# Input projection of a hybrid decoder layer: outputs with tokens on partitions, half of the contraction by Strassen's block scheme

## The chip, the cores and the metric

The kernel runs on one core of a Trainium2 chip. The metric is the device time of one execution in microseconds (us). Before the change the median of three runs is 696.79 us (696.76 to 697.26).

A core has five engines that work beside each other and meet at semaphores: TensorE (PE, matmuls; its weight loads are listed as PEld), VectorE (DVE), ScalarE (ACT), GpSimd (POOL) and SyncE (SP, which issues most transfers here). Matmul results go to PSUM, which has eight banks of 128 partitions x 512 fp32 words.

## The reference

One decoder layer on 256 tokens of width 2048, in fp32. The input projection is by far the largest product: 2048 x 11264 weights.

```python
h = rms_norm(x, norm_g)                                    # x: 256 x 2048
proj = h @ w_in                                            # 2048 x 11264
q, k, v, z_a, u_b, v_b, z_b, g_a, g_b = jnp.split(proj, cuts, axis=-1)   # seven of 1024, two of 2048
q, k = rms_norm(q, q_norm_g), rms_norm(k, k_norm_g)        # per head of 128, 8 heads
att = moba_attention(q, k, v)                              # 256 tokens: one block, causal softmax
y_a = (att * silu(z_a)) @ w_proj_a                         # 1024 x 2048
sgu = spatial_gating(gelu(u_b), gelu(v_b), ...)            # u * (W_s norm(v) + b), chunks of 128
y_b = (sgu * silu(z_b)) @ w_proj_b                         # 1024 x 2048
merged = sigmoid(g_a) * y_a + sigmoid(g_b) * y_b
return x + merged @ w_out                                  # 2048 x 2048
```

## The kernel before

**The weight stream.** All weights are laid out on the host as one stream of 120 granules of 128 x 2048 words (1 MB), in the order in which they are used (`schedule`). Granule i is loaded into a raw buffer by SP's queue (`load`, L96) three granules ahead, and split two granules ahead (`split`): ACT casts it to fp32r, the high half (wh, L120), and DVE subtracts the high half from the raw word, the low half (wl, L121), in two pieces of 1024 words. Every product of fp32 precision is then three fp32r products: low x high, high x high and high x low.

**Two kinds of granules.** For vb, v, q, k and out a *natural* granule holds 4 k tiles x 512 columns. The halves of x (or of the merged rows) are the stationary operand, the weights are moving, and the output has tokens on partitions (`mm_nat`, L233): 24 matmuls of 512 columns per granule, into two banks, one for each half of the tokens. For ub, zb, za, ga, gb and the two projections a *transposed* granule holds 16 k tiles x 128 columns. The weights are stationary, and x's two halves, side by side, are moving (`mm_tr`): one matmul of 512 columns with wh (L241) and one of 256 with wl (L243) for each k tile. The output then has columns on partitions, and ACT and DVE add its two parts (`tr_sum`, L248 and L250).

**x and its norm.** The layer's norm is not applied to x itself. x arrives transposed (`load_x`, L134), is multiplied by its gain and split into halves (`split_x`, L164 and L165). The rms of each token (rstd; R as a row) is applied after the product: as ACT's scale for natural outputs, by DVE (L372) for transposed ones.

**Order.** The stream runs vb, ub, v, q, k, zb, za, then 16 rounds of one tile of ga, one of gb and one of the projections, then out in four chunks of 512 columns. Work beside the stream (squares, transposes of q and k, scores, softmax, attention, spatial mixing) is hung on granule numbers with `at`. The framework turns this into one queue for each engine. It orders the instructions by priority and readiness, so an engine's order can differ from the text; each engine then executes its queue in order. Only the first splits are ordered by hand (`manual_schedule`).

**Buffers.** Three raw buffers, five half granules of wh and of wl; 14 general buffers of 2048 words; four banks of PSUM for accumulators and four for the rest.

Of the kernel before, what the change touches and what calls it, by code (L numbers as in the profile page):

```python
# [24 lines left out]
H = 8  # L25
# [3 lines left out]
WORDS = 2048  # L29
# [4 lines left out]
COLS = {"q": 0, "k": 1024, "v": 2048, "za": 3072, "ub": 4096, "vb": 5120, "zb": 6144,  # L34
        "ga": 7168, "gb": 9216}


def schedule():
    s = []

    def nat(name, c):
        s.extend(("nat", name, c, q) for q in range(4))

    def tr(name, j):
        s.append(("tr", name, j, 0))

    for c in range(2):
        nat("vb", c)
    for j in range(8):
        tr("ub", j)  # L50
    for name in ("v", "q", "k"):
        for c in range(2):
            nat(name, c)
    for name in ("zb", "za"):
        for j in range(8):
            tr(name, j)
    for j in range(16):
        tr("ga", j)
        tr("gb", j)
        s.append(("proj", "proj", j, 0))  # L60
    for c in range(4):
        nat("out", c)
    return s
# [3 lines left out]
def hybrid_layer_kernel(  # L67
# [6 lines left out]
    bs: bass.AP,  # L74
# [7 lines left out]
    big = ctx.enter_context(tc.tile_pool(name="big", bufs=14))  # L82
    wpool = ctx.enter_context(tc.tile_pool(name="wpool", bufs=3))
    work = ctx.enter_context(tc.tile_pool(name="work", bufs=2))
    small = ctx.enter_context(tc.tile_pool(name="small", bufs=4))
    ps_acc = ctx.enter_context(tc.tile_pool(name="ps_acc", bufs=4, space=bass.MemoryType.PSUM))
    ps_sd = ctx.enter_context(tc.tile_pool(name="ps_sd", bufs=4, space=bass.MemoryType.PSUM))
# [5 lines left out]
    raw, wh, wl = {}, {}, {}  # L93
# [3 lines left out]

    def load(i, pieces=1):
        if i >= NG:
            return  # L100
        raw[i] = wpool.tile([P, WORDS], F32, tag="raw", name=f"raw{i}")
        n = WORDS // pieces
        for a in range(pieces):
            load_piece(i, a * n, (a + 1) * n)

    HW = WORDS // 2

    def split(i, pieces=1, hs=range(2), js=None):
        if i >= NG:
            return  # L110
        n = HW // pieces
        for h in hs:
            if (i, h) not in wh:
                wh[i, h] = wpool.tile([P, HW], F32R, tag="wh", bufs=5, name=f"wh{i}_{h}")
                wl[i, h] = wpool.tile([P, HW], F32R, tag="wl", bufs=5, name=f"wl{i}_{h}")
            a, b = wh[i, h], wl[i, h]
            for j in js or range(pieces):
                sl = slice(j * n, (j + 1) * n)
                r = raw[i][:, h * HW + j * n:h * HW + (j + 1) * n]
                nc.scalar.copy(a[:, sl], r)  # L120
                nc.vector.tensor_tensor(b[:, sl], r, a[:, sl].bitcast(F32), op=ALU.subtract)  # L121

# [8 lines left out]
    xs = []

    def load_x(k0, k1):
        nc.sync.dma_start(xt[k0 // 8][:, k0 % 8:(k1 - 1) % 8 + 1, :],  # L134
                          xT[:, NV + k0 * S:NV + k1 * S].rearrange("p (k t) -> p k t", t=S))

    raw[0] = wpool.tile([P, WORDS], F32, tag="raw", name="raw0")
    nc.sync.dma_start(xv[:, 0:NV + S], xT[:, 0:NV + S])
    load_piece(0, 0, 512)
    nc.sync.dma_start(xv[:, NV + S:], xT[:, NV + S:NV + 2 * S])  # L140
# [8 lines left out]
    for i in range(4):  # L149
        xs.append(slot(F32R, f"xs{i}").rearrange("p (k c) -> p k c", c=512))  # L150

    warm = const.tile([P, 512], BF16, name="warm")
    nc.vector.memset(warm, 0.0)
    ps_w = ps_sd.tile([P, 512], F32, tag="sd", name="ps_w")
# [3 lines left out]
    def split_x(i, kks=range(4)):  # L158
        for kk in kks:
            k = 4 * i + kk  # L160
            src = x_k(k)
            g = vec[:, k:k + 1]
            hi = xs[i][:, kk, 0:S]
            nc.scalar.activation(hi, src, AF.Copy, scale=g)  # L164
            nc.vector.scalar_tensor_tensor(xs[i][:, kk, S:], src, g, hi.bitcast(F32),  # L165
                                           op0=ALU.mult, op1=ALU.subtract)
# [3 lines left out]
    ones = const.tile([P, 1], F32, name="ones")  # L170
    nc.gpsimd.memset(ones, 1.0)
    mhalf = const.tile([P, 8], F32, name="mhalf")
    nc.gpsimd.memset(mhalf, -0.5)
    tri_f = work.tile([P, 4, P], F32, tag="t2k", bufs=6, name="tri_f")
# [5 lines left out]
    wb = slot(F32, "wb").rearrange("p (a h t) -> p a h t", a=2, t=P)  # L180
    ws, bsb = wb[:, 0], wb[:, 1]

    def load_mix():
        nc.sync.dma_start(ws, wsT)
        nc.gpsimd.affine_select(out=ws, in_=ws, pattern=[[0, H], [1, P]], base=0,
                                channel_multiplier=-1, compare_op=ALU.is_ge, fill=0.0)
        nc.sync.dma_start(bsb, bass.AP(tensor=bs.tensor, offset=bs.offset,
                                       ap=[[0, P], [P, H], [1, P]]))
# [3 lines left out]
    sq = [slot(F32, f"sq{i}").rearrange("p (k t) -> p k t", t=S) for i in range(2)]  # L192
    ssum = work.tile([P, 2, S], F32, tag="t2k", bufs=6, name="ssum")

    def squares(i):
        if i == 0:
            nc.scalar.activation(sq[0][:, 0:2, :], xv[:, NV:].rearrange("p (k t) -> p k t", t=S), AF.Square)
            nc.scalar.activation(sq[0][:, 2:, :], xt[0][:, 2:, :], AF.Square)
        else:
            nc.scalar.activation(sq[i], xt[i], AF.Square)  # L200
        nc.vector.reduce_sum(ssum[:, i, :], sq[i].rearrange("p k t -> p t k"), axis=AX.X)
# [21 lines left out]
    def mm_nat(acc, lhs, i, q, by_row=False):  # L223
# [3 lines left out]
        for kk, m in order:  # L227
            k = 4 * q + kk
# [314 lines left out]
```

## Time and profile before

| | us |
|---|---|
| median of three runs | 696.79 |
| lowest and highest run | 696.76, 697.26 |
| span of the profiled execution | 695.3 |
| the profiled execution's own time | not listed apart from its span |
| PE busy in the span | 689.0 |
| DVE busy | 443.9 |
| ACT busy | 352.2 |
| mean transfer rate | 192 GB/s |

The span runs from the first to the last instruction of one execution; what lies around it is not in the profile. Busy times of the engines overlap, so they don't add up to the span. Matmuls are pipelined and their ends are modelled: a group's mean duration is longer than the distance from one matmul to the next, and this distance is the price in a full stream. The chain that ended last is followed back from the last instruction, at each step to what released it.

### The profile page before, as it was taken

Reading aid. Unit: us, or ns where it says so; the run is one execution under the profiler, and the core shown is the slowest. Engines: PE = TensorE matmul, PEld = TensorE weight load, DVE = VectorE, ACT = ScalarE, POOL = GpSimd, SP = SyncE. Lnnn points to the kernel's source line nnn. Section 1 sums busy time; section 2 is a strip of 40 time slices with the busy share of each in tenths; the row PEclk is TensorE's granted clock in tenths of the full one; section 3 lists DMA queues with packets and bytes.
Section 4 is the critical chain, followed back from the end, with each engine's and each line's share of the span. In section 5 each row is a group of like instructions: output and inputs, shape, how many; then the busy total and the mean of one; then the engine's idle time right before and its main releaser. Section 6 shows DMA issues by size and latency. Waiting matters only on the chain.

```text
span 695.3 us, 9323 instructions
## 1 busy us (share of the span) xinstructions
PE 689.0 (99%) x3638; PEld 591.6 (85%) x3638; DVE 443.9 (64%) x604; ACT 352.2 (51%) x522; POOL 22.6 (3%) x26
## 2 busy tenths in 40 slices
PE   8999999999999999999999999999999999999997
PEld 5888888888888889888888888888888888888886
DVE  5988555546566685866666666666666666654551
ACT  6854443344444496855644554455445445534330
POOL 1022000000111100000000000000000000000000
PEclk9999999999999999999999999999999999999999
DMA  8766554554555545445555555555545555557730
GB/s 309 296 249 235 182 187 176 182 186 181 196 184 189 182 154 209 156 153 199 194 182 181 186 186 201 195 201 184 182 182 187 194 199 200 190 181 247 251 138 30
DMA packets 21788, 133.77 MB, mean 192 GB/s; under 512 B 2417, under 2 KB 2929, under 8 KB 7025
## 3 DMA queue, kind: packets, MB, share of 16 engines
q1 hardware_dynamic: 20592, 131.09, 52.2%
q10 hardware_dynamic: 1152, 2.10, 1.0%
q8 instruction: 28, 0.46, 0.3%
q14 instruction: 16, 0.12, 0.0%
HBM read 131.08 MB, written 2.10 MB: 192 GB/s over the span
## 4 chain that ended last, share of the span: by engine, by line
PE 99%; DMA 1%; ACT 0%; DVE 0%; SPq 0%; DVEq 0%; issue 0%
PE acc_out L233 13%; PE acc_gb L241 8%; PE acc_ga L241 8%; PE acc_vb L233 7%; PE acc_v L233 6%; PE acc_q L233 6%; PE acc_k L233 6%; PE acc_ga L243 4%; PE acc_gb L243 4%; PE acc_ub L241 4%; PE acc_zb L241 4%; PE acc_za L241 4%; PE acc_pb L241 4%; PE acc_pa L241 4%; PE acc_pa L243 2%; PE acc_pb L243 2%
## 5 line engine op out<-in xcount | busy, mean ns | idle before, releaser
L121 DVE TENSOR_TENSOR wl<-raw,wh 128x1024 fp32r<-128x1024 f32 (+1 forms) x250 | 294.4, 1182 | 203.4 <-ACT wh L120 200.4
L120 ACT CAST wh<-raw 128x1024 fp32r<-128x1024 f32 (+1 forms) x250 | 253.2, 1018 | 302.1 <-PE acc_ga L241 44.5
L241 PE MATMUL acc_ga<-xs,wh 128*128 128x512 f32 x256 | 89.5, 391 | 0.0
L241 PE MATMUL acc_gb<-xs,wh 128*128 128x512 f32 x256 | 89.5, 391 | 0.0
L233 PE MATMUL acc_out<-wh,mT 128*128 128x512 f32 x256 | 78.8, 390 | 0.0
L243 PE MATMUL acc_gb<-xs,wl 128*128 128x256 f32 x256 | 71.8, 281 | 0.0
L243 PE MATMUL acc_ga<-xs,wl 128*128 128x256 f32 x256 | 71.8, 281 | 0.0
L241 PEld LDWEIGHTS acc_gb<-xs,wh 128*128 128x128 f32 x256 | 47.9, 187 | 10.4
L241 PEld LDWEIGHTS acc_ga<-xs,wh 128*128 128x128 f32 x256 | 47.9, 187 | 10.4
L233 PEld LDWEIGHTS acc_out<-wh,mT 128*128 128x128 f32 x256 | 48.0, 188 | 9.9
L233 PE MATMUL acc_out<-wl,mT 128*128 128x512 f32 x128 | 49.9, 390 | 0.0
L243 PEld LDWEIGHTS acc_gb<-xs,wl 128*128 128x128 f32 x256 | 48.5, 190 | 0.0
L243 PEld LDWEIGHTS acc_ga<-xs,wl 128*128 128x128 f32 x256 | 48.5, 190 | 0.0
L241 PE MATMUL acc_zb<-xs,wh 128*128 128x512 f32 x128 | 45.5, 399 | 0.0
L241 PE MATMUL acc_ub<-xs,wh 128*128 128x512 f32 x128 | 45.3, 399 | 0.0
L241 PE MATMUL acc_pb<-zbT,wh 128*128 128x512 f32 x128 | 45.1, 391 | 0.0
L241 PE MATMUL acc_pa<-zaT,wh 128*128 128x512 f32 x128 | 45.1, 391 | 0.0
L241 PE MATMUL acc_za<-xs,wh 128*128 128x512 f32 x128 | 44.6, 393 | 0.0
L233 PE MATMUL acc_vb<-wh,xs 128*128 128x512 f32 x128 | 41.2, 404 | 1.3 <-ACT wh L120 1.3
L233 PE MATMUL acc_v<-wh,xs 128*128 128x512 f32 x128 | 39.9, 393 | 0.0
L233 PE MATMUL acc_k<-wh,xs 128*128 128x512 f32 x128 | 39.6, 391 | 0.0
L233 PE MATMUL acc_q<-wh,xs 128*128 128x512 f32 x128 | 39.5, 390 | 0.0
(142 smaller groups left out, 1056.1 us busy)
## 6 DMA issues: line engine op xcount, KB each, us to landing
raw<-in_w SPq DMA_DIRECT2D x115, 1024.0 KB, 4.8
raw<-in_w SPq DMA_DIRECT2D x9, 512.0 KB, 7.9
xres<-in_x ACTq DMA_DIRECT2D x8, 256.0 KB, 7.1
out<-o SPq DMA_DIRECT2D x7, 256.0 KB, 6.5
xt<-in_xT SPq DMA_DIRECT2D x3, 512.0 KB, 8.2
raw<-in_w SPq DMA_DIRECT2D x2, 256.0 KB, 4.6
wb<-in_wsT SPq DMA_DIRECT2D x1, 512.0 KB, 5.7
wb<-in_bs SPq DMA_DIRECT2D x1, 512.0 KB, 7.5
```

Of the source, the lines that this page charges most:

```text
L120: nc.scalar.copy(a[:, sl], r)
L121: nc.vector.tensor_tensor(b[:, sl], r, a[:, sl].bitcast(F32), op=ALU.subtract)
L233: nc.tensor.matmul(acc[m], a, b[i, h][:, o:o + 512], start=(k == 0 and n == 0), stop=(k == KT - 1 and n == 2))
L241: nc.tensor.matmul(acc, wh[i, h][:, o:o + P], r, start=(kk == 0), stop=False, skip_group_check=True)
L243: nc.tensor.matmul(acc[:, 0:S], wl[i, h][:, o:o + P], r[:, 0:S], start=False, stop=(kk == nk - 1), skip_group_check=True)
```

## The change

The input projection is rebuilt. All outputs of it, and those of the projections, now have tokens on partitions.

- **Quads.** A quad is 1024 output columns: q, k, v, za, vb, ub, zb, and four quads of g, each with 512 columns of ga and 512 of gb. It has eight granules; granule kp holds k tiles kp and kp + 8 for two column blocks of 512, as blocks 12, 11, 22, 21 (first digit the half of k, second the column block). With two halves of the tokens there are four accumulators, one bank each. A *direct* granule does all eight block products (`direct`). In all quads but q, granules kp 0 to 3 are done by `seven`: seven block products, with four sums of weight blocks (t, built on DVE in `split`) and four forms of x blocks (`forms`). Four of the seven go to banks E and are combined by `early`, three go on in the accumulators L; `final` adds both. Quads take their granules in the order 4, 5, 0, 1, 6, 2, 3, 7. E and L change places from quad to quad.
- **Split.** A Strassen granule takes three additions on DVE (1024, 512 and 512 words), then casts and subtractions of 1536 and of 2048 words. Others take one cast and one subtraction of 2048.
- **Norm.** q is computed on x times its gain and scaled afterwards. In the meantime x is normalised, and all other quads use normalised x. For the statistics x is loaded a second time with tokens on partitions; ACT squares it.
- **Order.** q, k, v, za, vb, ub, zb, then four rounds of a g quad and four granules of the projections (512 columns), then out.
- **Work beside it.** Norms of heads use ACT's accumulators (`sums`). The softmax's denominator is applied with the gate, after attention. The gated results (`turn_z`) and the merged rows (`turn_m`) are transposed on PE.

```diff
+SK = (0, 1, 2, 3)
+MIXED = (4, 5, 0, 1, 6, 2, 3, 7)
+    quad("q", 0, PLAIN)
+    for name in ("k", "v", "za", "vb", "ub", "zb"):
+        quad(name, 0, MIXED)
     for c in range(4):
-        nat("out", c)
+        quad("g", c, MIXED)
+        s.extend(("proj", "proj", c, q, q) for q in range(4))
+    for c in range(4):
+        s.extend(("out", "out", c, q, q) for q in range(4))
...
+        t = wpool.tile([P, WORDS], F32, tag="raw", bufs=4, name=f"t{i}")
+        two = t[:, 0:2 * B].rearrange("p (a n) -> p a n", a=2)
+        nc.vector.tensor_tensor(two, r[:, B:3 * B].rearrange("p (a n) -> p a n", a=2),
+                                r[:, None, 0:B].to_broadcast([P, 2, B]), op=ALU.add)
+        nc.vector.tensor_tensor(t[:, 2 * B:3 * B], t[:, 0:B], r[:, 2 * B:3 * B], op=ALU.add)
+        nc.vector.tensor_tensor(t[:, 3 * B:], t[:, 2 * B:3 * B], r[:, 3 * B:], op=ALU.add)
+        wh[i] = wpool.tile([P, 3 * B], F32R, tag="whp", bufs=2, name=f"whp{i}")
+        wl[i] = wpool.tile([P, 3 * B], F32R, tag="wlp", bufs=2, name=f"wlp{i}")
+        halve(wh[i], wl[i], r[:, B:])
+        th[i] = wpool.tile([P, WORDS], F32R, tag="wh", bufs=3, name=f"th{i}")
+        tl[i] = wpool.tile([P, WORDS], F32R, tag="wl", bufs=3, name=f"tl{i}")
+        halve(th[i], tl[i], t)
...
+    xn = [slot(F32, f"xnat{m}") for m in range(2)]
+    for m in range(2):
+        nc.sync.dma_start(xn[m], x[m * P:(m + 1) * P, :])
...
+    def normalise(i):
+        src = xt[i]
+        nc.vector.tensor_tensor(src, src, R[:, None, :].to_broadcast([P, 8, S]), op=ALU.mult)
...
+        nc.vector.tensor_tensor(F[0], a22, a21, op=ALU.subtract)
+        nc.vector.scalar_tensor_tensor(F[1], F[0], -1.0, a11, op0=ALU.mult, op1=ALU.subtract)
+        nc.vector.tensor_tensor(F[2], a11, a21, op=ALU.subtract)
+        nc.vector.tensor_tensor(F[3], a12, F[1], op=ALU.add)
...
+        for acc, (hi, lo), (bh, bl) in ((L[0], A(1, 0), W("21")), (L[1], Fm(3), W("22")), (L[2], A(1, 1), T(3))):
+            three(acc, hi, lo, bh, bl, not started, False)
+        for acc, (hi, lo), (bh, bl) in ((E[0], A(0, 0), W("11")), (E[1], Fm(1), T(2)), (E[2], Fm(2), T(1)),
+                                       (E[3], Fm(0), T(0))):
+            three(acc, hi, lo, bh, bl, first, last)
+
+    def early(E, name):
+        c11, h, c22, c12 = (u(f"{name}_{n}") for n in ("c11", "h", "c22", "c12"))
+        nc.scalar.copy(c11, E[0])
+        nc.vector.tensor_tensor(h, E[1], c11, op=ALU.add)
+        nc.vector.tensor_tensor(c12, E[3], h, op=ALU.add)
+        nc.vector.tensor_tensor(h, E[2], h, op=ALU.add)
+        nc.vector.tensor_tensor(c22, E[3], h, op=ALU.add)
+        return c11, c12, h, c22
+
+    def final(L, e):
+        c11, c12, h, c22 = e
+        nc.vector.tensor_tensor(c11, L[0], c11, op=ALU.add)
+        nc.vector.tensor_tensor(c12, L[1], c12, op=ALU.subtract)
+        nc.vector.tensor_tensor(h, L[2], h, op=ALU.add)
+        nc.vector.tensor_tensor(c22, L[3], c22, op=ALU.subtract)
+        return [[c11, c12], [h, c22]]
+
+    def sums(C, name):
+        for m in range(2):
+            for c in range(2):
+                ss = small.tile([P, 4], F32, tag="ss", bufs=8, name="ss")
+                junk = u("junk")
+                for h in range(4):
+                    nc.scalar.activation(junk[:, h * P:(h + 1) * P], C[m][c][:, h * P:(h + 1) * P], AF.Square,
+                                         accum_out=ss[:, h:h + 1])
+                rs = small.tile([P, 4], F32, tag="rs", bufs=8, name="rs")
+                rsqrt(rs, ss, 4, P)
+                X["rs", name, m, c] = rs
...
+    def merge(c, Y):
+        g = X["g", c]
+        for m in range(2):
+            nc.vector.tensor_tensor(g[m][0], Y[m], g[m][0], op=ALU.mult)
+        for m in range(2):
+            nc.vector.tensor_tensor(g[m][1], Y[2 + m], g[m][1], op=ALU.mult)
+            nc.vector.tensor_tensor(g[m][0], g[m][0], g[m][1], op=ALU.add)
...
+    at(i0 + 4, normalise, 1)
+    at(i0 + 4, halves_x, 1)
+    at(i0 + 5, normalise, 0)
+    at(i0 + 5, forms)
+    at(i0 + 6, halves_x, 0)
+    at(i0 + 6, halves_f)
```

## Rows read from the trace of the kernel before

**Rows 1.** The page: engines, busy us (share of the span) x instructions.
```profile
PE 689.0 (99%) x3638; PEld 591.6 (85%) x3638; DVE 443.9 (64%) x604; ACT 352.2 (51%) x522; POOL 22.6 (3%) x26
```

**Rows 2.** The page: chain that ended last, by engine.
```profile
PE 99%; DMA 1%; ACT 0%; DVE 0%; SPq 0%; DVEq 0%; issue 0%
```

**Rows 3.** That chain in order of time: start us, us, what.
```profile
6.11 34.88 PE acc_vb L233 x144
...
53.31 0.24 PE acc_ub L241
...
97.83 10.94 PE acc_v L233 x48
108.77 0.89 PE ps_m L359 x8
...
145.04 32.64 PE acc_q L233 x144
177.68 0.87 PE ps_qT L292 x8
...
604.41 87.09 PE acc_out L233 x384
691.53 0.42 DVE o L407
```

**Rows 4.** Timeline of DVE, 240 to 259 us: start us, us, instruction.
```profile
240.43 0.69 DVE L266 TENSOR_TENSOR q<-gk 128x512 f32<-128x512 f32 x1
241.15 0.69 DVE L268 TENSOR_REDUCE ss<-q 128x4 f32<-128x512 f32 x1
...
257.13 1.23 DVE L121 TENSOR_TENSOR wl<-raw,wh 128x1024 fp32r<-128x1024 f32 x1
258.27 0.42 DVE L250 TENSOR_TENSOR t_zb<-acc_zb,lo_zb 128x256 f32<-128x256 f32 x1
258.61 1.22 DVE L121 TENSOR_TENSOR wl<-raw,wh 128x1024 fp32r<-128x1024 f32 x1
```

**Rows 5.** Groups by line and shape: DVE's halving, ACT's square of 2048.
```profile
L121 DVE TENSOR_TENSOR wl<-raw,wh 128x1024 fp32r<-128x1024 f32 x230 | 281.4, 1225 | 199.2 <-ACT wh L120 196.2 <-PE ps_m L359 2.9
...
L200 ACT ACTIVATE sq<-xt 128x2048 f32<-128x2048 f32 x1 | 1.9, 1902 | 0.0
```

**Rows 6.** Timeline of ACT, 252 to 253 us: two exponentials with accumulators.
```profile
252.35 0.40 ACT L324 ACTIVATE prob<-S,nm 128x128 f32<-128x128 f32 x1
...
252.75 0.39 ACT L324 ACTIVATE prob<-S,nm 128x128 f32<-128x128 f32 x1
```

**Rows 7.** Waits: engine, line, waited for; us in total, times, longest us.
```profile
DVE wl L121 <- ACT wh L120: 200.4, 188, 2.4
```

**Rows 8.** Windows: us, PE, PEld, DVE, ACT, POOL busy (count), clock, DMA share, GB/s.
```profile
0.00:10.00 10.00, 7.48 (x17) 4.11 (x18) 3.12 (x7) 4.78 (x8) 2.43 (x11) 1.00 0.73 230
10.00:20.00 10.00, 10.00 (x45) 8.19 (x45) 9.50 (x19) 9.37 (x22) 0.00 (x0) 1.00 1.03 414
20.00:30.00 10.00, 10.00 (x46) 8.29 (x45) 9.94 (x14) 10.00 (x15) 0.00 (x0) 1.00 0.95 376
...
330.00:605.00 275.00, 275.00 (x1588) 242.71 (x1587) 184.40 (x266) 139.66 (x219) 0.00 (x0) 1.00 0.53 189
```

**Rows 9.** Timeline of all engines, 6 to 10 us.
```profile
6.11 1.22 PE L233 MATMUL acc_vb<-wh,xs 128*128 128x512 f32 x2 [1.27 <-ACT wh L120]
...
7.56 1.05 PE L233 MATMUL acc_vb<-wh,xs 128*128 128x512 f32 x2
...
8.41 0.63 PE L233 MATMUL acc_vb<-wl,xs 128*128 128x512 f32 x1
...
9.19 0.62 ACT L120 CAST wh<-raw 128x512 fp32r<-128x512 f32 x1 [0.71 <-DMA raw<-in_w]
```

More of the change, by code (lines that the diff above doesn't have):

```diff
@@ L131, in hybrid_layer_kernel @@
[L131 to L138, printed above, removed]
+                halve(wh[i][:, sl], wl[i][:, sl], r[:, sl])
+            return
+        t = wpool.tile([P, WORDS], F32, tag="raw", bufs=4, name=f"t{i}")
+        two = t[:, 0:2 * B].rearrange("p (a n) -> p a n", a=2)
@@ new lines, in halves_f, with three @@
+    def halves_f():
+        nonlocal Fh, Fl
+        Fh = slot(F32R, "Fh").rearrange("p (a k t) -> p a k t", a=4, t=P)
+        Fl = slot(F32R, "Fl").rearrange("p (a k t) -> p a k t", a=4, t=P)
+        nc.scalar.copy(Fh, Fs)
+        nc.vector.tensor_tensor(Fl, Fs, f(Fh), op=ALU.subtract)
+    def three(acc, hi, lo, bh, bl, start, stop, first=False):
+        order = ((lo, bh), (hi, bh), (hi, bl))
+        if first:
+            order = ((hi, bh), (lo, bh), (hi, bl))
+        for n, (a, b) in enumerate(order):
+            nc.tensor.matmul(acc, a, b, start=(start and n == 0), stop=(stop and n == 2))
@@ new lines, in hybrid_layer_kernel, with direct @@
+    BLK = {"12": 0, "11": 1, "22": 2, "21": 3}
+    def direct(L, hs, ls, i, kp, start, stop):
+        t, a = kp // 4, 2 * (kp % 4)
+        for c in range(4):
+            r, col = c // 2, c % 2
+            for kh in range(2):
+                hi = hs[t][:, a + kh, r * P:(r + 1) * P]
+                lo = ls[t][:, a + kh, r * P:(r + 1) * P]
+                o = BLK[f"{kh + 1}{col + 1}"] * B
+                three(L[c], hi, lo, wh[i][:, o:o + B], wl[i][:, o:o + B], start and kh == 0, stop and kh == 1,
+                      first=(i == 0))
@@ new lines, in mix @@
+    def mix(banks):
+        for c in range(2):
+            for m in range(2):
+                vn = X["vb"][m][c]
+                ps = bank(banks[2 * c + m], f"ps_m{c}{m}")
+                for j in range(4):
+                    sl = slice(j * P, (j + 1) * P)
+                    nc.tensor.matmul(ps[:, sl], X["ws"][c][:, sl], vn[:, sl], start=True, stop=True)
+                for j in range(4):
+                    sl = slice(j * P, (j + 1) * P)
+                    g = KT + 2 + 4 * c + j
+                    nc.scalar.activation(vn[:, sl], ps[:, sl], AF.Identity, bias=vec[:, g:g + 1])
@@ new lines, in hybrid_layer_kernel, with at, aux @@
+    later = {}
+    def at(i, fn, *a):
+        later.setdefault(i, []).append((fn, a))
+    free = {}
+    def aux(fn, *a, n0=0, n1=4):
+        fn(*a, free["banks"][n0:n1])
+    i0 = first["q", 0]
+    at(i0 + 2, stats)
+    at(i0 + 3, stats_row)
+    at(i0 + 4, normalise, 1)
[4 more added lines that the diff above has]
+    at(i0 + 6, halves_f)
+    i0 = first["k", 0]
+    at(i0 + 1, sums, None, "q")
+    at(i0 + 3, norm_qk, "q")
@@ new lines, in hybrid_layer_kernel @@
+    i0 = first["v", 0]
+    at(i0 + 0, turn_qk, "q", None)
+    at(i0 + 1, sums, None, "k")
+    at(i0 + 3, norm_qk, "k")
+    i0 = first["za", 0]
+    at(i0 + 0, turn_qk, "k", None)
+    at(i0 + 1, score, None)
+    at(i0 + 2, softmax, 0)
+    at(i0 + 2, softmax, 1)
+    i0 = first["vb", 0]
+    at(i0 + 0, turn_p, 0, None)
+    at(i0 + 0, turn_p, 1, None)
+    at(i0 + 0, func, "za", AF.Silu)
+    at(i0 + 1, attend, 0, None)
+    at(i0 + 1, attend, 1, None)
+    at(i0 + 3, load_mix)
+    i0 = first["ub", 0]
@@ L524 @@
     xs = x[0]
+    pair = [kp + 8 * h for kp in range(8) for h in range(2)]
     ins = {
```

643 lines of the change are left out of this document (319 added, 324 removed).

## Prediction

> **What bounds the kernel now.** I read the engines' totals first, then the chain that ended last, then that chain in order of time. PE is busy 99% of the span, DVE 64%, ACT 51% [rows 1], and the chain is PE for 99% of its length [rows 2]. So the kernel lasts as long as its stream of matmuls, and the price of one is the distance from one to the next, not the modelled duration. In order of time [rows 3]: 384 matmuls of 512 columns take 87.09 us in the output stage, 0.2268 each, and 144 take 32.64 in q, the same. A transposed pair (512 and 256 columns) costs 0.348: from the first of acc_ub to the first of acc_v lie 44.52 us and 8 tiles of 16 pairs. Eight transposes take 0.87 (0.109 each). Eight records of ps_m, which are four fp32 products of 128 columns, take 0.89 (0.2225 each).
>
> These prices rebuild the span. 1152 natural matmuls (vb, v, q, k, out) x 0.2268 = 261.3; 1152 pairs x 0.348 = 400.9; 58 transposes 6.3; 24 score, 16 mixing and 24 attention products (counted in 128 columns) x 0.2225 = 14.2; the start 6.1, and 2.2 more because the first 144 take 34.88 instead of 32.64 [rows 3]; from the last chain piece on PE to the end 3.8. Sum 694.8, span 695.3. The runs' median is 696.79, 1.5 above the span, which I carry over unchanged; the profiled execution's own time is not listed apart.
>
> **What PE gains.** A quad is 1024 output columns against 16 k tiles, in eight granules. A direct granule has 4 outputs x 2 k tiles x 3 = 24 matmuls, a Strassen granule 7 x 3 = 21. q is direct: 192. Ten mixed quads (k, v, za, vb, ub, zb, four g) have 4 x 21 + 4 x 24 = 180 each: 1800. The two projections, now natural, have 384, the output 384. Together 2760 x 0.2268 = 626.0. Transposes rise from 58 to 122 (za and zb 32, merged rows 32 more): 13.3. The fp32 products stay at 64: 14.2. With the same start and end (12.1) that is 665.6, or 29.2 less than 694.8. If PE stayed the only bound the span would be 666.1. Of the 29.2, 27.2 come from the 120 matmuls saved, 9.0 from leaving the pairs (1152 x 0.348 against 1728 x 0.2268), and 7.0 go to the transposes.
>
> **What DVE and ACT get.** DVE issues [rows 4] show 1.14 from a 1024 element operation to the next, 0.34 for 256, so about 0.61 for 512, 1.67 for 1536, 2.21 for 2048, and 0.72 for 512 where the next one needs the result. The mean duration, 1.225 for 1024 [rows 5], has a tail in which the next one already runs. A direct granule costs DVE 2.21 (before, two halves of 1.14). A Strassen granule has three chained additions (1024, 512, 512), a subtraction of 1536 and one of 2048: 1.25 + 0.72 + 0.61 + 1.67 + 2.21 = 6.46. The last needs ACT's cast of the 2048 sums, about 1.9 by the 2048 element square of [rows 5], which starts only after the additions, while the 1536 subtraction covers 1.67: some 0.4 of waiting, so 6.85. A mixed quad takes DVE 4 x 6.85 + 4 x 2.21 + early 2.66 (2 x 0.61 + 2 x 0.72) + final 2.44 = 41.3; PE needs 180 x 0.2268 = 40.8. Two engines are now at the bound.
>
> The smaller work changes little in this balance. In k to zb DVE gets 20.9 (four predicated copies 2.4, maxima 3.5, some 20 tiny ones at 0.17, attention and the norm of vb 16 x 0.21 each, za's halves and the spatial product 2.4 each), PE 22.0 (72 transposes, 64 products). Six quads: PE 6 x 40.8 + 22.0 = 266.8, DVE 6 x 41.3 + 20.9 = 268.7.
>
> *Lateness inside a quad.* PE's end of the quad before is zero. final ends at 2.5; s0 is ready at 9.35 and wanted after two direct granules at 10.9; s1 is ready at 16.2 and wanted at 15.65, 0.55 late; d6 is in time; s2 at 25.25 against 26.4; s3 at 32.1 against 31.15, 0.95 late. Early then waits for PE anyway. So 1.5 per quad, 9 for six, if the order is that of the text. It need not be: the queues are ordered by readiness (in [rows 4] halving, tr sums and products alternate), and an addition of the next granule can fill the 0.4. Bounds 0 and 9; I take 4.5.
>
> *Entry.* In the last granules of q DVE also normalises x, builds the four forms and their halves: 2 x 2.2, 4 x 0.65 and 3 x 2.2, 13.6, with five splits and the first Strassen split, about 29.5 against 27.3 of PE (five granules). Bounds 0 and 4; I take 3.
>
> *Bursts on ACT.* sums issues 16 squares with their accumulators, 0.40 apart as the exponentials are now [rows 6], 6.4 us, three times; the softmax some 7; the two norms of q and k and the mixing some 5 each. DVE, in order, has about 4.8 us to do meanwhile (a 2.21 subtraction, 2.6 of additions), less the 1.4 of the cast behind the burst. Exposed: (6.4 - 3.4) x 3 + 3.6 + 3 x 1.4, some 16 to 17; lower bound 0, if ACT runs ahead. DVE already waits 188 times for ACT's casts, 2.4 at the longest [rows 7], but with 200 us to spare; I take 5, nearer the lower end because ACT has about a quarter of each quad free.
>
> *The g rounds.* PE 40.8 + 96 x 0.2268 = 62.6, DVE 41.3 + four splits 8.8 + merge 3.9 = 54, so DVE catches up in the projection granules. In the text's order merge stands before s0: s1 is 2 late, s3 0.7. Upper 10 for four, lower 0; I take 3.
>
> *Start.* Ahead of granule 3 the sync queue now carries x a second time, by rows: 2.1 MB. Transfers ran at 230, 414 and 376 GB/s in the first three 10 us windows [rows 8], 6.4 MB by 20 us. Before, granule 3 is the 6.3rd MB; after, the 8.4th, at 25 us. Cast and subtraction bring it to 29.2, its 24 matmuls to about 34.4; before, four granules end at 41.0 - 10.9 = 30.1. So 4.3 later. The first granule needs the second half of its words early, since the first output takes blocks 11 and 21; that half lands at 9.2 [rows 9], which the same delay covers. Bounds 2 and 8.
>
> The new row loads, xres on ACT's queue, four raw buffers shared with the sums, the bank swap and POOL's small powers I cost at nothing: PE has two granules (10 us) in hand where a 1 MB transfer takes about half that, and bank swaps wait only for early and final, already counted. If that cover is gone they are in the upper bounds.
>
> Sum: 666.1 + 4.3 + 4.5 + 3 + 5 + 3 = 685.9; with 1.5 around it **687.4**. All lower ends give 669.6, all upper ones about 715.
>
> **The clock.** In the start two matmuls take the 0.85 us from 7.56 to 8.41 [rows 9], 0.43 each, and in the 10 us from 10 on there are 45 [rows 8], 0.22 each: the two levels 1.2 and 2.4 GHz by their columns, although the granted clock is printed as 1.00 for both stretches. Before the slow ones PE had waited 1.27 us for its first cast [rows 9]. The rest of the span shows no second fall, but PE also has no idle time there. The Trainium skill, "TensorE: Matmul & The Clock Gate", section on HAM oscillation, says that idle gaps between matmul bursts return the array to half its clock. The waits worked out above are a microsecond or two and no row shows what such gaps do in mid-span, so it is a rival with a small chance and no term of the sum.
>
> **Rivals.** (a) PE stays the only bound, DVE's lateness hides: 669 to 676. For it: totals of 266.8 and 268.7 are equal and ACT has room. DVE was 95 to 99% busy from 10 to 30 us and PE did not stop [rows 8]. Against it: outside of the start DVE is at 67% in the long window of [rows 8], so no row shows it feeding PE through a whole stage when full. Chance 0.14. (b) The other side: DVE becomes the bound, because each Strassen granule is a chain DVE, ACT, DVE and any ACT delay stands in it unhidden. Every mixed quad then takes 42.3 and more plus its small work, and entry, bursts and g rounds stand near their upper ends: 704 to 712. It decides from (29.2 - 4.3) / 10 = 2.5 us of lateness per mixed quad. For it: six quads without spare time on DVE. Against: the granule order spreads Strassen granules with direct ones between. Chance 0.25. (c) The clock falls after the waits: one granule per mixed quad at 0.43 instead of 0.227 costs 21 x 0.2 = 4.3, ten times 43: 730. Chance 0.05. (d) Gain and lateness cancel, within 0.2%: 0.08. That the seven products are not issued can't be; the loops are literal.
>
> **How the numbers follow.** My forecast, 676 to 695, has 0.48. Faster by over 0.2% (1.4 us, about what a measurement of this kernel can tell) is 0.48 + 0.14 = 0.62; same 0.08; slower 0.25 + 0.05 = 0.30. The range 671 to 709 leaves out the clock, the worst of (b) and the best of (a), under 2 in 10. The forecast's own range is 676 to 695.
>
> **What would show it.** Right: about 2760 matmuls of 512 columns 0.227 apart; PE still over 95% of the chain; DVE over 90% busy from k to zb; PE's waits naming DVE's subtraction of the sums (tl) or ACT's cast (th), first at s1 and s3; mixed quads of 41 to 43 us plus their small work; granule 3 some 4 us later. Wrong: mixed quads over 45, waits for the casts of th in runs after sums and softmax, or matmuls 0.43 apart after a wait. If no wait names DVE, (a) holds.

## The result and the profile after

The kernel after takes 693.02 us (692.55 to 693.12), the kernel before 696.79. The ratio is 0.9941, 95% interval 0.9927 to 0.9956, so the change gains 3.8 us. The forecast of 687.4 had the direction right and the size wrong: 9.4 us were expected. The profiled span is 691.2 us (695.3 before).

The engines' totals and the chain by engine, to be held against [rows 1, 2], say what kind of kernel it is now.

```profile
PE 664.2 (96%) x3018; PEld 547.6 (79%) x3018; DVE 553.6 (80%) x498; ACT 388.9 (56%) x453; POOL 37.0 (5%) x28
...
PE 85%; DVE 8%; DMA 2%; issue 2%; ACT 2%; POOL 1%; SPq 0%; DVEq 0%; ACTq 0%
```

DVE has gone from 64% to 80% of the span, and PE from 99% to 85% of the chain. In the windows view the columns after the length are busy time (and instructions) of PE, PEld, DVE, ACT and POOL, then the granted clock, the DMA share and GB/s. The first three rows answer to [rows 8]; the fourth spans v to zb.

```profile
0.00:10.00 10.00, 3.59 (x8) 1.03 (x8) 0.27 (x1) 2.19 (x3) 2.41 (x10) 1.00 0.76 238
10.00:20.00 10.00, 0.00 (x0) 0.00 (x0) 0.00 (x0) 3.15 (x8) 0.00 (x0) 1.00 1.03 420
20.00:30.00 10.00, 8.20 (x25) 6.14 (x26) 7.57 (x8) 10.00 (x16) 0.00 (x0) 1.00 0.84 308
...
112.00:341.00 229.00, 229.00 (x1109) 191.65 (x1108) 216.81 (x225) 152.73 (x229) 26.45 (x13) 1.00 0.49 187
```

From v to zb PE never stops and DVE is busy for 216.8 of 229 us, 95%. The surprise is the second row: from 10 to 20 us PE does nothing at all. In [rows 3] PE's first product came at 6.1; in the chain after, in order of time, it comes at 21.76:

```profile
8.32 10.21 DMA xt<-in_xT
18.97 1.29 ACT xt L191 x3
20.76 0.95 ACT wh L120
21.76 1.22 PE acc_q L275 x2
...
85.31 2.30 DVE tl L121
88.15 4.34 PE seven_k L275 x12
```

**By stage.** The first product of each accumulator marks where a stage begins. The first column is that of q, the next ones the time from a stage's first product to the next stage's, the last the g rounds after the first quad, with their projections. The line "PE alone" is the prediction's price for PE's work (192 x 0.2268 = 43.55 and two transposes for q, 180 x 0.2268 = 40.8 for a mixed quad, and the small PE work inside a stage); to q the prediction's sum adds the 2.2 us of [rows 3].

```
                   first q |  q     k     v     za    vb    ub    zb    g0  | rest of g
PE alone              6.1  | 43.8  40.8  42.6  47.9  48.8  42.6  44.4  40.8 | 213.9
after                21.8  | 46.5  44.5  42.8  48.0  48.8  43.3  44.5  45.0 | 213.9
e1  cast first        8.3  | 49.5  45.5  43.7  48.2  48.8  43.1  45.2  45.0 | 213.9
e3  row loads late    8.5  | 49.2  42.2  45.0  48.1  48.9  44.7  45.2  45.0 | 213.9
e4  addition twice   21.6  | 45.9  44.7  48.8  50.9  49.0  51.2  47.7  48.1 | 214.5
e8  three Strassen    8.7  | 49.3  42.8  43.3  48.7  49.7  43.3  45.1  41.5 | 216.6
e10 cast, then scale  9.2  | 51.2  43.0  43.7  48.0  48.8  43.3  44.5  45.1 | 213.9
```

The span is 25.1 us over PE alone (691.2 against 666.1). The table finds 15.7 of it ahead of the first product, 3.7 in k, 4.2 in the first g quad, and 1.7 in five smaller losses (0.5 of it in q); the rest is rounding. Nothing is lost in vb or in the last three g rounds.

**Why PE starts late.** ACT's timeline of the first 23 us (start, duration, line, operation; in brackets the idle time before it and what ended it):

```profile
5.21 0.91 ACT L191 ACTIVATE xt<-xt,vec 128x256 f32<-128x256 f32 x2
14.72 1.70 ACT L191 ACTIVATE xt<-xt,vec 128x256 f32<-128x256 f32 x4 [8.60 <-DMA xt<-in_xT]
18.55 1.70 ACT L191 ACTIVATE xt<-xt,vec 128x256 f32<-128x256 f32 x4 [2.13 <-DMA xt<-in_xT]
20.16 0.60 ACT L194 CAST xuh<-xt 128x512 fp32r<-128x512 f32 x1
20.67 1.99 ACT L120 CAST wh<-raw 128x1024 fp32r<-128x1024 f32 x2
```

ACT executes its queue in order, as these rows show: it stands idle for 8.60 us although what the cast of L194 reads is there. After the two scalings of x's first pair of k tiles stand eight scalings of later pairs, which wait 8.60 and 2.13 us for their pieces of x. Only behind them come the first cast of x and the first cast of weights, without which there is no product. The waits view has the consequence in one line:

```profile
PE acc_q L275 <- ACT wh L120: 16.9, 1, 16.9
```

Before the change the scaling itself wrote the high half of x, so no cast stood between them. The diff makes the scaling write x in place and adds a cast that reads it on the same engine. That the framework filled the gap between these two with scalings that it took to be ready earlier is my reading of the order, not something a run shows.

### The profile page after: what moved, and what is told of

It is laid out like the page before. It is cut to its first block, busy times and chain, and to the rows that moved or that the text cites. A ratio compares the mean times of both kernels' runs of the same rounds, so it can differ in the third digit from the quotient of the medians.

```text
span 691.2 us, 7699 instructions
## 1 busy us (share of the span) xinstructions
PE 664.2 (96%) x3018; PEld 547.6 (79%) x3018; DVE 553.6 (80%) x498; ACT 388.9 (56%) x453; POOL 37.0 (5%) x28
## 4 chain that ended last, share of the span: by engine, by line
PE 85%; DVE 8%; DMA 2%; issue 2%; ACT 2%; POOL 1%; SPq 0%; DVEq 0%; ACTq 0%
PE acc_g L275 14%; PE y L275 13%; PE acc_out L275 13%; PE seven_g L275 5%; PE acc_ub L275 4%; PE acc_v L275 4%; PE acc_q L275 4%; PE acc_za L275 4%; PE acc_vb L275 4%; PE acc_zb L275 4%; DMA xt<-in_xT 2%; PE acc_k L275 2%; DVE wl L121 2%; PE seven_v L275 2%; PE seven_ub L275 2%
## 5 line engine op out<-in xcount | busy, mean ns | idle before, releaser
L121 DVE TENSOR_TENSOR wl<-raw,wh 128x2048 fp32r<-128x2048 f32 (+1 forms) x82 | 182.7, 2236 | 65.6 <-ACT wh L120 65.3
L120 ACT CAST wh<-raw 128x2048 fp32r<-128x2048 f32 (+1 forms) x82 | 153.0, 1870 | 106.5 <-PE acc_out L275 42.2
L120 ACT CAST th<-t 128x2048 fp32r<-128x2048 f32 x40 | 76.5, 1912 | 105.6 <-DVE t L141 105.5
L121 DVE TENSOR_TENSOR tl<-t,th 128x2048 fp32r<-128x2048 f32 x40 | 92.0, 2301 | 28.2 <-ACT th L120 27.6
L120 ACT CAST whp<-raw 128x1536 fp32r<-128x1536 f32 x40 | 59.1, 1480 | 34.5 <-DMA raw<-in_w 16.2
L121 DVE TENSOR_TENSOR wlp<-raw,whp 128x1536 fp32r<-128x1536 f32 x40 | 70.1, 1752 | 0.0
L275 PE MATMUL acc_g<-wh,xh 128*128 128x512 f32 x128 | 49.8, 389 | 0.0
L275 PE MATMUL acc_g<-wh,xl 128*128 128x512 f32 x128 | 49.7, 389 | 0.0
L138 DVE TENSOR_TENSOR t<-raw 128x1024 f32<-128x1024 f32 x40 | 48.8, 1221 | 0.6
L275 PE MATMUL acc_g<-wl,xh 128*128 128x512 f32 x128 | 48.8, 389 | 0.0
L140 DVE TENSOR_TENSOR t<-t,raw 128x512 f32<-128x512 f32 x40 | 27.8, 694 | 0.3
L141 DVE TENSOR_TENSOR t<-t,raw 128x512 f32<-128x512 f32 x40 | 27.4, 686 | 0.3
```

The lines of the kernel that those rows point to most:

```text
L120: nc.scalar.copy(h, r)
L121: nc.vector.tensor_tensor(l, r, f(h), op=ALU.subtract)
L138: nc.vector.tensor_tensor(two, r[:, B:3 * B].rearrange("p (a n) -> p a n", a=2), r[:, None, 0:B].to_broadcast([P, 2, B]), op=ALU.add)
L140: nc.vector.tensor_tensor(t[:, 2 * B:3 * B], t[:, 0:B], r[:, 2 * B:3 * B], op=ALU.add)
L141: nc.vector.tensor_tensor(t[:, 3 * B:], t[:, 2 * B:3 * B], r[:, 3 * B:], op=ALU.add)
L275: nc.tensor.matmul(acc, a, b, start=(start and n == 0), stop=(stop and n == 2))
```

## The experiments

Theory S: the 13 to 16 us at the start are this order on ACT. Its rival T: they are transfers (x's rows, 2.1 MB more, ahead of the weights), and any order would wait. Theory D: after the start DVE and PE are both at the bound, so each us on DVE shows. Its rival P: PE alone bounds, and DVE has slack.

**e1: the casts first.** The scalings of a pair, its casts and the casts of a granule are kept in the order of the text on ACT.

```diff
-            split_x(i + 4)
-        load(i + 3, pieces=2 if i < 2 else 1)
-        split(i + 2)
+            with tc.manual_schedule(engines={mybir.EngineType.Activation}), tc.issue_after(last):
+                split_x(i + 4)
+                load(i + 3, pieces=2 if i < 2 else 1)
+                split(i + 2)
+            last = getattr(cast[-1], "ins", cast[-1])
```

(`last` is the latest cast; `stats` is ordered behind it too; from i = 4 on the text is as it was.)

> Edit: ACT's order in the first four granules is tied to the text, so the casts of granules 0 and 1 stand ahead of the scalings of x for k tiles 8 to 15, and the squares of x stand behind the cast of granule 4. Theory (order on ACT): PE's first product starts near 8 to 9 us instead of 21.8, the late pieces of x and raw3 are then the next limit by some 4 us, and the total falls by 9 to 14, to 679 to 684. Rival (bytes: the second load of x and the later pieces arrive too late whatever ACT does): PE's start moves, but its fifth granule still ends near 52, and the total falls by less than 3.

Measured 685.49 us (685.28 to 685.73), ratio 0.9833 (0.9816 to 0.9849). With the transfers of the start issued as in the kernel after, the order on ACT moves the first product from 21.8 to 8.3 and gains 7.5 us: S holds, with less gain than the 9 to 14 that I had expected. ACT's timeline of e1:

```profile
5.33 0.91 ACT L193 ACTIVATE xt<-xt,vec 128x256 f32<-128x256 f32 x2
6.27 0.62 ACT L196 CAST xuh<-xt 128x512 fp32r<-128x512 f32 x1
7.25 1.04 ACT L122 CAST wh<-raw 128x1024 fp32r<-128x1024 f32 x1 [0.36 <-DMA raw<-in_w]
```

But 13.4 us at the start became 7.9 in the span. q takes 49.5 instead of 46.5, since PE, once early, overtakes the transfers. The chain of e1 begins with loads of weights, and the waits name the cast behind them:

```profile
4.77 8.15 DMA raw<-in_w
12.94 12.63 DMA raw<-in_w
```

```profile
PEld acc_q L277 <- ACT wh L122: 5.0, 3, 4.4
```

So T is right about a remainder: against PE alone, 2.2 us of later start and 3.5 of q beyond its 46.0, some 6 together. Against the kernel after, q gives back 3.0 and k to g0 another 2.6 (319.5 us in e1, 316.9 there). A reading that no run isolates: the late start had given DVE a lead over PE. It isn't the only one, since the compiled queues of ACT, DVE and PE in e1 differ from those of the kernel after again in later stages (DVE's between 150 and 275 us).

**e2: e1, and x's rows behind the first weights.** The two row loads move from ahead of granule 3 to behind granules 3 and 4.

```diff
-    xn = [slot(F32, f"xnat{m}") for m in range(2)]
-    for m in range(2):
-        nc.sync.dma_start(xn[m], x[m * P:(m + 1) * P, :])
+    xn = []
...
         load(i + 3, pieces=2 if i < 2 else 1)
+        if i < 2:
+            xn.append(slot(F32, f"xnat{i}"))
+            nc.sync.dma_start(xn[i], x[i * P:(i + 1) * P, :])
```

> The edit of the run before, and the two 1 MB loads of x by rows issued behind the weights of granules 3 and 4 instead of ahead of them. Theory: with ACT's order mended, the bytes ahead of granule 3 are the next limit, so this gains 2 to 4 us more, unless the row statistics then come later than they are needed and give it back. Rival (granule 3 is not waited for): within 1 us of the run before.

Measured 684.26 us, ratio 0.9812 (0.9798 to 0.9827): 1.2 us less than e1, as q falls from 49.5 to 48.1 and k from 45.5 to 43.0 while v rises by 1.9 and ub by 1.7. I had expected 2 to 4; the extra transfer costs little.

**e3: the row loads alone.** The edit of e2 without that of e1.

> Only the two loads of x by rows are moved behind the weights of granules 3 and 4; ACT's order stays as it was. Theory (order on ACT): PE still starts behind the scaling of the last tiles of x, at 18 to 20 us, because these pieces share the transfer engines with less; the total falls by 1 to 4 us. Rival (bytes): the whole late start goes, 9 us or more.

Measured 684.64 us, ratio 0.982 (0.9805 to 0.9834). PE starts at 8.5, where I had expected 18 to 20. This doesn't speak for T, because the moved loads changed the compiled order too. In e3's timeline of ACT the cast of weights now stands ahead of the later scalings:

```profile
6.23 0.62 ACT L192 CAST xuh<-xt 128x512 fp32r<-128x512 f32 x1
7.44 1.04 ACT L120 CAST wh<-raw 128x1024 fp32r<-128x1024 f32 x1 [0.59 <-DMA raw<-in_w]
9.31 1.05 ACT L120 CAST wh<-raw 128x1024 fp32r<-128x1024 f32 x1 [0.82 <-DMA raw<-in_w]
10.26 0.90 ACT L189 ACTIVATE xt<-xt,vec 128x256 f32<-128x256 f32 x2
```

Two experiments that look alike in the text differ on the chip by an order that neither text shows; for the start only e1 holds the transfers still. The short edit of e3 is the base of e5, e7 and e8.

**e4: 0.72 us more on DVE in each Strassen granule.** The kernel after, with the second addition written twice.

```diff
         nc.vector.tensor_tensor(t[:, 2 * B:3 * B], t[:, 0:B], r[:, 2 * B:3 * B], op=ALU.add)
+        nc.vector.tensor_tensor(t[:, 2 * B:3 * B], t[:, 0:B], r[:, 2 * B:3 * B], op=ALU.add)
```

> The changed kernel with one of the three additions on DVE (512 words, 0.72 us with the next one depending on it) done twice in each of the 40 Strassen granules: 28.8 us more on DVE, nothing else. Theory (DVE and PE are both at the bound, DVE 95% busy from the second quad to the sixth): the quads from k to zb pay most of their 17 us and the g rounds little, so 10 to 20 us more in all. Rival (PE alone is the bound after the start, DVE's work is hidden): less than 5 us more. Other rival (DVE is the bound everywhere): 26 us or more.

Measured 717.52 us, ratio 1.0288 (1.0273 to 1.0303). Forty additions are 28.8 us more on DVE, and the total grows by 24.5. P falls. D holds in its direction but not in its size: 24.5 is more than the 10 to 20 that I had expected, close to the 26 of a DVE that bounds everywhere. Nor does each us on DVE show. Every mixed quad got the same 2.9 us, and the price is 6.0 in v, 2.9 in za, 7.9 in ub, 3.2 in zb and 3.1 in g0, but nearly nothing in k, in vb and in the last g rounds (0.6 for three). By the waits below, what counts is whether the addition falls into the chain DVE, ACT, DVE that PE waits for. Two things are mixed in: the compiled queues differ from those of the kernel after in many places, and the granted clock is 0.97 in v and in ub and 0.93 in g0, which by these figures is at most some 6 us (an estimate). PE now waits where it had not:

```profile
PEld acc_ub L276 <- ACT th L120: 5.9, 3, 2.7
...
PEld acc_v L276 <- ACT th L120: 4.8, 2, 2.6
```

**e5: the gates' products on POOL.** e3, with the eight products of the spatial gate and of zb moved off DVE.

```diff
-                nc.vector.tensor_tensor(X["ub"][m][c], X["ub"][m][c], X["vb"][m][c], op=ALU.mult)
+                nc.gpsimd.tensor_tensor(X["ub"][m][c], X["ub"][m][c], X["vb"][m][c], op=ALU.mult)
...
-                nc.vector.tensor_tensor(X["zb"][m][c], X["zb"][m][c], X["ub"][m][c], op=ALU.mult)
+                nc.gpsimd.tensor_tensor(X["zb"][m][c], X["zb"][m][c], X["ub"][m][c], op=ALU.mult)
```

> On the kernel with the late loads of x by rows (e3): the spatial product and the gate of the second branch, eight products of 512 words in zb and the first g quad, go from DVE to POOL: 4.9 us less on DVE there. Theory (DVE is the bound up to the first g quad, where the changed kernel loses 4.2 us): that quad falls from 45.0 to 41 or 42 and the total by 3 to 4 us. Rival (the loss there is ACT's table loads and casts): less than 1 us.

Measured 691.27 us, ratio 0.9915 (0.9898 to 0.9932): 6.6 us slower than e3 with less work on DVE, where I had expected 3 to 4 us less. zb takes 50.7 instead of 45.2. The timelines of POOL, DVE and PE of e5 in zb show why:

```profile
294.73 1.45 POOL L454 TENSOR_TENSOR ub_c<-ub_c,vb_c 128x512 f32<-128x512 f32 x1 [22.61 <-ACT vb_c L449]
296.14 1.74 POOL L454 TENSOR_TENSOR ub_h<-ub_h,vb_h 128x512 f32<-128x512 f32 x1
297.83 2.82 POOL L454 TENSOR_TENSOR ub_c<-ub_c,vb_c 128x512 f32<-128x512 f32 x1
```

```profile
293.30 1.75 DVE L121 TENSOR_TENSOR wlp<-raw,whp 128x1536 fp32r<-128x1536 f32 x1
294.97 1.76 DVE L140 TENSOR_TENSOR t<-t,raw 128x512 f32<-128x512 f32 x1
296.65 2.85 DVE L121 TENSOR_TENSOR wlp<-raw,whp 128x1536 fp32r<-128x1536 f32 x1
299.42 1.78 DVE L141 TENSOR_TENSOR t<-t,raw 128x512 f32<-128x512 f32 x1
...
303.47 0.69 DVE L140 TENSOR_TENSOR t<-t,raw 128x512 f32<-128x512 f32 x1
```

```profile
306.42 0.79 PE L273 MATMUL acc_zb<-tl,xh 128*128 128x512 f32 x1 [2.44 <-DVE tl L121]
```

Beside a POOL product each DVE instruction is 1.1 us longer than alone (the last DVE row, and the first, at whose very end POOL begins). It isn't slowed evenly: each of the three ends its usual distance after a POOL product ends. POOL ends at 296.18, 297.88 and 300.65; DVE 0.55 later (a 512 addition goes at 0.6), 1.62 later (its 1536 subtraction at 1.67) and 0.55 later. POOL's second and third product in turn end 1.15 after the DVE instruction before them. So DVE waits for POOL's instruction and then does its own. The Trainium skill, "SBUF — State Buffer", section "SBUF: two separate sides", says the same: a DVE operation with two operands in SBUF and a GpSimd operation hold one pair of ports in turn, the later one blocked until the first has finished. In zb the sums of a granule are late by it, and PE waits 2.44 us for tl. From 307.0 us on twelve matmuls then go 0.43 apart instead of 0.227, and the granted clock of 308 to 316 us is 0.72: 2.4 of zb's 5.5 us are clock.

**e7: the first addition on POOL.** e3, with the addition of 1024 words moved.

```diff
-        nc.vector.tensor_tensor(two, r[:, B:3 * B].rearrange("p (a n) -> p a n", a=2),
+        nc.gpsimd.tensor_tensor(two, r[:, B:3 * B].rearrange("p (a n) -> p a n", a=2),
```

> On e3: the first of the three additions of every Strassen granule (1024 words) goes from DVE to POOL, 1.14 us less on DVE in each of 40 granules. Theory (DVE at the bound): the lateness of the quads from k to the first g, about 12 us in e3, falls by half or more, the total by 4 to 9 us. Rival (the chain, not DVE's busy time, is the bound: POOL's addition is slower and stands at the head of the chain): no gain, or slower by up to 10 us.

Measured 724.07 us, ratio 1.0386 (1.037 to 1.0401), 39.4 over e3, although DVE loses 45 us of work (40 x 1.13); I had expected 4 to 9 us less, and of the rival no more than 10 us. The groups by line (busy time, mean ns) of e3, then of e7, and the wait of e7 that took the place:

```profile
L138 DVE TENSOR_TENSOR t<-raw 128x1024 f32<-128x1024 f32 x40 | 49.3, 1232 | 0.7 <-DMA raw<-in_w 0.2
```

```profile
L138 POOL TENSOR_TENSOR t<-raw 128x1024 f32<-128x1024 f32 x40 | 124.5, 3112 | 402.1 <-DVE wl L121 119.1 <-DMA raw<-in_w 101.2 <-DVE t L141 79.2
```

```profile
DVE t L140 <- POOL t L138: 66.0, 27, 3.3
```

POOL takes 2.5 times as long and holds DVE up, and the chain DVE, ACT, DVE of a Strassen granule now begins on the slowest engine. DVE is busy 202.8 of 252 us from v to zb and PE still waits: the order of a granule's steps counts, not only an engine's total. The granted clock is 0.96 over the 355 us from k to g0, so at most some 14 of the 39.4 us are clock (an estimate).

**e8: three Strassen granules of eight instead of four.** e3, with one pair of k tiles made direct.

```diff
-SK = (0, 1, 2, 3)
+SK = (0, 1, 2)
```

> On e3: three granules of each mixed quad by Strassen's scheme instead of four (k tiles 3 and 11 done directly). PE gets 10 x 3 matmuls more, 6.8 us; DVE gets 4.3 us less in each quad. Theory (DVE and PE both at the bound, some 12 us of lateness from k to the first g quad): the lateness nearly goes, so the total stays within 4 us of e3, up or down. Rival (PE alone is the bound): 6 to 7 us slower than e3.

Measured 682.83 us (682.23 to 682.99), ratio 0.9796 (0.9782 to 0.9811), the lowest of all: 1.8 under e3, within the 4 that I had expected, and 10.2 under the kernel after. (Against 1.8 stand 0.8 us between two runs of one and the same order, e10 and e12 below.) PE has 30 matmuls more, 6.8 us, and DVE 4.3 us less in each quad. The gain is in g0, 45.0 to 41.5, which is PE's own 180 + 3 matmuls (41.5) with no loss, and in v and ub (1.7 and 1.4); k, za, vb and the rest of g pay. From v to zb, row of e3, then of e8:

```profile
100.00:332.00 232.00, 228.90 (x1102) 190.09 (x1101) 216.09 (x226) 152.42 (x228) 21.73 (x13) 1.00 0.49 184
```

```profile
101.00:331.00 230.00, 230.00 (x1117) 193.69 (x1116) 199.55 (x209) 148.40 (x225) 14.95 (x13) 1.00 0.50 186
```

With DVE at 87% PE stops nowhere. Where g0 of the kernel after lost 4.2 is in its DVE timeline:

```profile
359.71 2.29 DVE L121 TENSOR_TENSOR tl<-t,th 128x2048 fp32r<-128x2048 f32 x1 [1.44 <-ACT th L120]
...
371.92 2.29 DVE L121 TENSOR_TENSOR tl<-t,th 128x2048 fp32r<-128x2048 f32 x1
374.13 0.68 DVE L141 TENSOR_TENSOR t<-t,raw 128x512 f32<-128x512 f32 x1
376.83 2.29 DVE L121 TENSOR_TENSOR tl<-t,th 128x2048 fp32r<-128x2048 f32 x1 [2.02 <-ACT th L120]
```

Where two Strassen granules follow each other, the sums of the second are done last and DVE idles for the whole cast, 2.02 us instead of the 0.4 that I had worked out: its 1536 subtraction, which was to cover the cast, had been issued ahead of the additions. Two neighbours alone don't cost it: in e8 the first pair of them stays, DVE has less to do, and g0 loses nothing.

**e9, e10: the first 5 MB in the order of use.** e9 is e2 with granule 0 whole, then each piece of x with the granule that needs it. e10 is e9 with the casts of a granule ahead of the next scalings.

```diff
     load_piece(0, 512, 1024)
-    load_x(2, 4)
     load_piece(0, 1024, WORDS)
-    load_x(4, 8)
+    load_x(2, 4)
     load(1, pieces=2)
-    load_x(8, 12)
+    load_x(4, 8)
     load(2, pieces=2)
+    load_x(8, 12)
     load_x(12, 16)
```

```diff
-                split_x(i + 4)
                 load(i + 3, pieces=2 if i < 2 else 1)
...
                 split(i + 2)
+                split_x(i + 4)
```

> On e2 (ACT's order tied to the text, x by rows late): the pieces of x and of the first granules are loaded in the order in which the granules want them, granule 1 ahead of k tiles 4 to 15. In e2 PE waits 4.3 us for the cast of granule 1. Theory (transfers ahead of granule 1 are what is left of the late start): that wait goes, q falls by 3 to 4 us, the total by 2 to 4. Rival (DVE's chain through the row statistics sets the end of q and k anyway): the total falls by less than 1 us, and the time reappears in k and v.

> On e9: in the first four granules the cast of the weights stands ahead of the scaling of a later pair of k tiles on ACT, so that granule 2 no longer waits for the piece of x with k tiles of pairs 4 and 5. In e9 this wait is 4.5 us. Theory (the rest of the late start is the same thing as its first part, ACT in order behind a late piece of x): the wait goes, q falls from 49.2 by 3 to 4 us, the total to 679 to 681. Rival (the time comes back in k and v, because DVE's chain through the row statistics does not move): the total stays at 682.5 to 684.

Measured 683.65 us, ratio 0.981 (0.9795 to 0.9824), and 684.14 us, 0.9812 (0.9795 to 0.983), within 0.6 us of e2, as the rivals had it. The wait only moves. e10 waits for the cast of weights and, at 33 to 36 us, for something new, the norm of the tokens:

```profile
PEld acc_q L275 <- ACT wh L122: 5.2, 1, 5.2
...
PEld ps_R L235 <- POOL rstd L225: 4.0, 1, 4.0
```

The transposes of rstd stand in PE's queue. What the start loses beyond the order on ACT these reorderings did not lower; that the transfers bound it is argued from the waits, not shown by a run.

**e11, e12: two variants of e10.** e11 has SK = (0, 1, 2). e12 has the squares of q and its norm three granules later.

```diff
-    at(i0 + 1, sums, None, "q")
-    at(i0 + 3, norm_qk, "q")
+    at(i0 + 4, sums, None, "q")
+    at(i0 + 6, norm_qk, "q")
```

> The kernel of the run before with three Strassen granules in each mixed quad instead of four. Theory (DVE and PE at the bound in turn): 1 to 4 us less than the run before, as between e3 and e8 (1.8). Rival (with the start mended DVE has room again): 3 to 7 us more.

> On e10: the squares of q and its norm on ACT, which stand in the first Strassen granules of k and wait there for POOL's powers, come three granules later. Theory (a burst on ACT in the Strassen granules delays the casts of the sums, and DVE and PE with them): k or v lose 1 to 3 us less. Rival (bursts are hidden): within 1 us of e10.

e11: 685.05 us, ratio 0.9833 (0.9818 to 0.9849), 0.9 over e10, with intervals that overlap, where e8 had gained 1.8 over e3 and I had expected 1 to 4. Its g0 falls to 41.5 as in e8, but q takes 52.0 and za and vb 1.5 and 0.8 more; v and ub, where e8 gained, had lost only 1.1 and 0.7 in e10. Why q, which has no Strassen granule, grows by 0.8 is open. So three Strassen granules gain on the base of e3 and show no gain on that of e10.

e12: 683.37 us, 0.9806 (0.9789 to 0.9824), 0.8 under e10 with intervals that overlap. It decides nothing about the burst, because the edit didn't reach the chip: in their traces ACT, DVE, POOL and PE execute the same instructions in the same order in e10 and e12. The squares of q begin 1.4 us after k's first product in both, and the norm of q waits for POOL as before, 1.71 us in both. The row is of e12:

```profile
71.63 2.16 ACT L351 ACTIVATE q<-q,rs 128x128 f32<-128x128 f32 x7 [1.71 <-POOL rs L225]
```

The framework orders by readiness, and a later place in the text didn't change that. What e12 does show is that 0.8 us lies between two runs of one order.

## Why the prediction was wrong in size

**PE's gain: right.** The price of 0.2268 per matmul and the count hold. The last three g rounds and the projections take 213.9 us, the price to a tenth, and vb takes its 48.8.

**The step that failed is *Start*.** It worked out 4.3 us from the bytes that the sync queue carries ahead of granule 3, with bounds of 2 and 8, and it assumed that ACT would follow the transfers as before. Measured: 15.7 to the first product and 0.5 more in q, twice the upper bound. It gave the added cast of x no line of its own and never walked ACT's queue: the new cast reads what the scaling before it has written, and eight scalings that wait for later transfers stood in between. The transfers' part by itself was nearly right: e1, with ACT's order put right and the transfers untouched, starts 2.2 late and loses 3.5 in q, 5.7 against 4.3. And e1's total, 685.49, lies 1.9 under the 687.4 forecast: with the start as I had taken it, the sum would have held, though in part by luck, as 1.4 more at the start stands against 3.9 less lateness (11.6 from k to g0). In the kernel after two errors pull against each other as well: 11.9 more at the start, 6.4 less lateness.

**Lateness: 15.5 forecast in four terms, 9.1 measured** (the losses of the kernel after from k to g0, against PE alone).

- *Inside quads*, 4.5: 1.2 over v, za, vb, ub and zb. DVE's total was near (252.3 us busy from k to zb; 268.7 worked out, with 9.6 of waits in it), and the order by readiness fills the gaps, as the lower bound had it. But little slack is left, as e4 shows.
- *Entry*, 3, and *bursts*, 5: together 3.7 in k. (By its own prices the sum in *Entry* is 31.1, not 29.5; its bounds of 0 and 4 hold it.) What ended last there is a norm on ACT that had waited for POOL, and behind it the cast of the sums. The rows are of ACT, then of DVE, in k:

```profile
81.32 2.16 ACT L351 ACTIVATE q<-q,rs 128x128 f32<-128x128 f32 x7 [1.71 <-POOL rs L225]
```

```profile
85.31 2.29 DVE L121 TENSOR_TENSOR tl<-t,th 128x2048 fp32r<-128x2048 f32 x1 [4.28 <-ACT th L120]
```

  The prediction had costed POOL's powers at nothing; here the four of q take POOL 6.93 us, and the norm behind them holds up the cast of the sums. The squares themselves were cheaper than forecast, 0.29 apart and not 0.40. Of the 3.7, 1.6 are clock (see (c) below), which leaves some 2.1 for this wait. In e10 and e12 the same wait of DVE is 4.30 and 4.29, the clock in k stays at 1.00, and k loses 2.2 and 2.4. That is what the traces show; no run took the norm out of the way. In the stages of k's and vb's squares and of the softmax PE loses little (0.3, 0.7 and 0.1), so ACT does run ahead there.
- *g rounds*, 3: 4.2, all in the first. The other three lose nothing, since DVE catches up in the projections as argued; g0 comes straight from zb with DVE at its limit, and in its two pairs of neighbouring Strassen granules DVE waits 1.44 and 2.02 us for a cast. e8, with less on DVE, loses nothing there.

**The rivals.** (a), PE alone, is refuted by e4. (b), DVE as the bound at 2.5 us of lateness per mixed quad, stayed at 0.9; e4, at 0.72 us more per Strassen granule, is what it would have looked like. (c), the clock, occurred once behind the start. In k PE waited 1.59 us for that subtraction; soon after, the matmuls go 0.43 apart, the level of 1.2 GHz, and the granted clock of 86 to 90 and 90 to 94 us is 0.79:

```profile
87.65 0.50 PE L275 MATMUL acc_k<-tl,xh 128*128 128x512 f32 x1 [1.59 <-DVE tl L121]
...
88.99 0.63 PE L275 MATMUL seven_k<-th,Fl 128*128 128x512 f32 x1
89.42 0.63 PE L275 MATMUL seven_k<-th,Fh 128*128 128x512 f32 x1
...
91.86 0.39 PE L275 MATMUL seven_k<-th,Fh 128*128 128x512 f32 x1
92.09 0.40 PE L275 MATMUL seven_k<-tl,Fh 128*128 128x512 f32 x1
```

Seven matmuls at 0.43 instead of 0.227 and two at a third of a us are 1.6 us, part of k's 3.7. A wait of 1.72 us in g0 was followed by no fall:

```profile
359.73 0.50 PE L275 MATMUL acc_g<-th,xl 128*128 128x512 f32 x1 [1.72 <-ACT th L120]
```

In e4, with more waits, a stretch in the first g quad runs mostly at the lower level, granted clock 0.54 (the eighth column), part of e4's 24.5 us:

```profile
380.00:385.00 5.00, 4.20 (x9) 2.98 (x10) 4.22 (x2) 5.00 (x4) 0.00 (x0) 0.54 0.52 205
```

So the rule of the Trainium skill that the prediction quoted, "TensorE: Matmul & The Clock Gate" on HAM oscillation, showed in the kernel after at one of three such waits (1.59, 1.72 and 1.40 us), and cost 1.6 us there. In e1 PE waits five times for 1.4 to 1.8 us from 28 us on, and the granted clock stays at 1.00.

**The signs named in advance.** DVE over 90% from k to zb: seen (252.3 of 272 us). PE's waits naming tl or th: seen, but far fewer than one per quad. Quads of 41 to 43 us and their small work: all but k and the first of g. PE over 95% of the chain: 85%. Granule 3 some 4 us later: the whole stream was 16 us later.

## What to carry to other kernels

When a step is split so that a second instruction on the same engine reads the first one's result, walk that engine's compiled queue through the start: what stands between the two, and what transfer does it wait for? Where two engines are both near full, it can pay to take work off the one with the longer chain even at a price on the other: 6.8 us more of matmuls gave a kernel 1.8 us faster on one base (e8) and none on another (e11). Moving work from DVE to POOL can cost DVE time. And an edit of the text is not yet an edit of the queue: e3 changed an order that it didn't name, and e12 left the order that it named as it was.

## What the runs showed of the hardware that was not expected

- A POOL product beside a DVE subtraction of two SBUF operands makes DVE wait for POOL's instruction: 2.85 us for 1.75, 1.78 for 0.69 (e5). The same addition of 1024 words takes 3.11 us on POOL beside a busy DVE and 1.23 on DVE (e7, e3).
- A wait of 1.59 us on PE in mid-span was followed by seven matmuls at half rate; one of 1.72 us, and five of 1.4 to 1.8 us in e1, were not.
